# Choosing experts head by head beside the top-k, with part of the selection on GpSimd

## The chip, the cores and the metric

The kernel runs on one core of a Trainium2 chip. The metric is the device time of one execution in microseconds (us). PE is TensorE (matmuls), DVE is VectorE, ACT is ScalarE, POOL is GpSimd, and SP issues most transfers. A line number such as L541 is a line of the kernel before; where the changed kernel is quoted, the numbers are its own.

## What is computed

One decoder block on 512 tokens of width 1024, in float32: RMS norm, an input projection, a causal convolution branch and a sliding-window attention branch merged by gates, an output projection, a second RMS norm, and then a channel mixer that picks experts by product keys. The change touches that mixer only. Per token and head (8 heads) two score rows over 128 keys are formed, the best 16 of each are kept, the best 16 of the 256 sums are chosen, and the chosen experts' rows of two tables of 16,384 x 1024 are used:

```python
q = (h @ w_pq).reshape(B, S, PEER_HEADS, 2, PEER_DHALF)
sc = jnp.einsum("bshcd,hcnd->bshcn", q, sub_keys)
s_top, i_top = lax.top_k(sc, PEER_TOPK)
cand = s_top[..., 0, :, None] + s_top[..., 1, None, :]
cand_idx = i_top[..., 0, :, None] * N_KEYS + i_top[..., 1, None, :]
best, pos = lax.top_k(cand.reshape(...), PEER_TOPK)
expert_idx = jnp.take_along_axis(cand_idx.reshape(...), pos, axis=-1)
gate = jax.nn.softmax(best, axis=-1)
a = jax.nn.gelu(jnp.einsum("ced,cd->ce", u_emb[idx], hx), approximate=False)
out = jnp.einsum("ce,ced->cd", g * a, v_emb[idx])
```

## The kernel before

The 512 tokens are 4 blocks of 128 tokens, one token per partition. Block 0 gathers its experts' rows by indirect DMA from GpSimd's queue (`by_rows`, `gathered`, L600). Blocks 1 to 3 are "dense": for them all 16,384 experts are multiplied out, 128 at a time. One **up-projection** (`u_step`, L635 to L641) loads a table block of 128 experts (`wraw`), ACT rounds it to `whi` (L120), DVE forms the remainder `wlo` (L122), PE runs 24 matmuls of 384 columns (L130 to L132), and ACT takes the GELU. Of 128 up-projections 31 are due before the second table starts.

The stretch around the change has two parts.

The **top-k part** (`scores`, `head`): for each of 16 score rows (8 heads x 2) PE forms the query and the scores, and DVE finds the best 16 for the four blocks: MAX8 (L482), FIND_INDEX8 (L483), MATCH_REPLACE8 (L484), then both once more (L485, L486). After every second row `head` builds 80 candidate sums per token (`cand`, L504 to L510, two buffers) and takes their best 16: values into `bv`, positions into `bp`.

The **choosing and building part**: for each dense block `choose(b)` turns positions into experts, and `build_g(b)` writes a gate table to memory. `choose` computes from `bp`, with 11 small DVE instructions on 128 elements (8 heads x 16), which of the 16 first keys (`c_i`) and of the 16 second keys (`c_j`) each winner used. It then looks the key numbers up without a gather. It compares the position with 0 to 15 (`eq`, L539), multiplies with the key numbers (L541) and sums over 16 (`sel`, L542), on tiles of 4 heads x 16 x 16 = 1024 elements:

```python
tt(eq, src[:, hs, :, None].to_broadcast(wide), iota[...].to_broadcast(wide), op=OP.is_equal)
nc.vector.tensor_tensor(eq, eq, sif[:, hs, s, None, :].to_broadcast(wide), op=OP.mult)
nc.vector.tensor_reduce(r[:, hs], eq, axis=AX.X, op=OP.add)
```

That is 4 such triples per block, 16 in all, every one on DVE. The result gives the row index for gathers (`c_e`, `eidx`, L544 and L545) and, for dense blocks, the key numbers split into a high part, a low part and a second key, transposed into `keyT`. `build_g` then makes, per group of 16 tokens, one-hot operands on DVE (`xa`, `xb`, two `yt` at L584 and two `xt` at L587 of 1024 elements), multiplies them on PE (L592, the histogram matmuls), and ACT moves the result to `gst` (L594). A dense block has 8 groups, so there are 24. One up-projection is emitted after each group.

The order of the instructions on each engine is not the order of this text: a list scheduler with its own model of durations places every instruction when the kernel is built, keeps each engine's queue in that order, and sets the waits. So up-projections, top-k and choosing are interleaved on DVE. The pools are single or double buffered as the `bufs` say; a buffer's next writer waits for its last reader.

Of the kernel before, what the change touches and what calls it, by code (L numbers as in the profile page):

```python
# [21 lines left out]
NB = S // P  # L22
# [15 lines left out]
CAND = 80  # L38
# [13 lines left out]
LOW = 16  # L52
# [27 lines left out]
def body(ctx: ExitStack, tc: tile.TileContext, a, out):  # L80
    nc = tc.nc
# [9 lines left out]
    def psum(tag):  # L91
        return ps.tile([P, S], F32, name=tag, tag=tag, bufs=2)
# [12 lines left out]
    iota = const.tile([P, P], F32, name="iota")  # L105
# [71 lines left out]
    def chunk(b):  # L177
        return slice(b * P, (b + 1) * P)
# [223 lines left out]
    p = psum("ot")  # L402
# [4 lines left out]
    for j in range(KB):  # L407
# [4 lines left out]
        else:  # L412
            nc.scalar.activation(sq, y[:, j], AF.Square)
            nc.vector.tensor_tensor(ysum, ysum, sq, op=OP.add)
    p = psum("ot")
    nc.tensor.matmul(p, ones, ysum, start=True, stop=True)
    r = rstd_of(p, D, [fr.tile([P, S], F32, name="ln_v", tag="qs", bufs=2),
                       fr.tile([P, S], F32, name="ln_t", tag="sg"),
                       fr.tile([P, S], F32, name="ln_r", tag="qs", bufs=2)])
# [7 lines left out]
    for j in range(KB):  # L427
        p = mm_block(a["w_ao"][j], oT)
        nc.vector.tensor_tensor(sga[:, j], sga[:, j], p, op=OP.mult)
    mT = pair_y("m")  # L430
    for j in range(KB):
        p = mm_block(a["w_co"][j], yT)
# [11 lines left out]
    for b0 in range(0, NB, 2):  # L444
        acc = [psum(t) for t in (("ot", "ot", "sc", "sc") if b0 == 0 else ("sc", "sc", "mm", "mm"))]
        for k in range(KB):
            hi, lo = load_w(a["w_out"][k])
            for c in range(2):
                for n in range(2):
                    ns = slice(n * 512, (n + 1) * 512)  # L450
                    p, cs = acc[2 * c + n], chunk(b0 + c)
# [3 lines left out]
        for c in range(2):  # L455
            b = b0 + c
# [11 lines left out]
    eidx = rp.tile([P, NB, SLOTS], U32, name="eidx")  # L468
# [5 lines left out]
    rt = gctx.enter_context(tc.tile_pool(name="rt", bufs=1, reuse_waits="tile"))  # L474
    sv = rt.tile([P, NB, 16, TOPK], F32, name="sv")
    si = rt.tile([P, NB, 16, TOPK], U32, name="si")
    bv = rt.tile([P, NB, HEADS, TOPK], F32, name="bv")
    bp = rt.tile([P, NB, HEADS, TOPK], U32, name="bp")

    def top16(vals, idx, src, n):  # L480
        w = rt.tile([P, P], F32, name="topw", bufs=2)[:, :n]
        nc.vector.max(vals[:, 0:8], src)  # L482
        nc.vector.max_index(idx[:, 0:8], vals[:, 0:8], src)  # L483
        nc.vector.match_replace(w, vals[:, 0:8], src, -3.0e38)  # L484
        nc.vector.max(vals[:, 8:16], w)  # L485
        nc.vector.max_index(idx[:, 8:16], vals[:, 8:16], w)  # L486

    def scores(hc):
        if hc == 0:
            early[:] = halves([a["w_pq"][0], a["w_pq"][1]], tT)  # L490
        p = early[hc] if hc < 2 else mm_block(a["w_pq"][hc], tT)
        sk = rt.tile([P, P], F32, name="sk", bufs=2)
        nc.sync.dma_start(sk, a["subk"][hc])
        q = rt.tile([P, S], F32, name="pq", bufs=2)
        nc.scalar.activation(q, p, AF.Copy)
        p = psum("sc")
        for b in range(NB):
            nc.tensor.matmul(p[:, chunk(b)], q[:, chunk(b)], sk, start=True, stop=True)
        for b in range(NB):
            top16(sv[:, b, hc], si[:, b, hc], p[:, chunk(b)], KEYS)  # L500

    def head(h):
        s1, s2 = sv[:, :, 2 * h], sv[:, :, 2 * h + 1]
        cand = rt.tile([P, NB, CAND], F32, name="cand", bufs=2)  # L504
        nc.vector.tensor_tensor(cand[:, :, 0:16], s1[:, :, 0:1].to_broadcast([P, NB, 16]), s2, op=OP.add)
        nc.vector.tensor_tensor(cand[:, :, 16:72].rearrange("p b (i j) -> p b i j", j=8),
                                s1[:, :, 1:8, None].to_broadcast([P, NB, 7, 8]),
                                s2[:, :, None, 0:8].to_broadcast([P, NB, 7, 8]), op=OP.add)
        nc.vector.tensor_tensor(cand[:, :, 72:80], s1[:, :, 8:16], s2[:, :, 0:1].to_broadcast([P, NB, 8]),
                                op=OP.add)  # L510
        for b in range(NB):
            top16(bv[:, b, h], bp[:, b, h], cand[:, b], CAND)

    def choose(b):
        sh = [P, HEADS, TOPK]
        t = {n: rt.tile(sh, F32, name="c_" + n) for n in ("p", "q", "r", "t", "e", "i", "j")}
        u = rt.tile(sh, U32, name="c_u")
        ts, tt, stt = nc.vector.tensor_scalar, nc.vector.tensor_tensor, nc.vector.scalar_tensor_tensor
        nc.vector.tensor_copy(t["p"], bp[:, b])
        ts(u, bp[:, b], 3, None, op0=OP.logical_shift_right)  # L520
        nc.vector.tensor_copy(t["q"], u)
        ts(u, bp[:, b], 7, None, op0=OP.bitwise_and)
        nc.vector.tensor_copy(t["r"], u)
        ts(t["i"], t["q"], -1.0, 0.0, op0=OP.add, op1=OP.max)
        ts(t["t"], t["p"], -72.0, 0.0, op0=OP.add, op1=OP.max)
        tt(t["i"], t["i"], t["t"], op=OP.add)
        ts(t["t"], t["q"], 1.0, 8.0, op0=OP.is_equal, op1=OP.mult)
        stt(t["j"], t["q"], 9.0, t["r"], op0=OP.is_lt, op1=OP.mult)
        tt(t["j"], t["j"], t["t"], op=OP.add)
        sif = rt.tile([P, HEADS, 2, TOPK], F32, name="sif")  # L530
        nc.vector.tensor_copy(sif, si[:, b].rearrange("p (h c) k -> p h c k", c=2))
        wide = [P, HEADS // 2, TOPK, TOPK]
        sel = []
        for s, src in ((0, t["i"]), (1, t["j"])):
            r = rt.tile(sh, F32, name=f"sel{s}")
            for h0 in (0, HEADS // 2):
                hs = slice(h0, h0 + HEADS // 2)
                eq = rt.tile(wide, F32, name="eq")
                tt(eq, src[:, hs, :, None].to_broadcast(wide), iota[:, None, None, :TOPK].to_broadcast(wide),  # L539
                   op=OP.is_equal)  # L540
                nc.vector.tensor_tensor(eq, eq, sif[:, hs, s, None, :].to_broadcast(wide), op=OP.mult)  # L541
                nc.vector.tensor_reduce(r[:, hs], eq, axis=AX.X, op=OP.add)  # L542
            sel.append(r)
        stt(t["e"], sel[0], float(KEYS), sel[1], op0=OP.mult, op1=OP.add)  # L544
        nc.vector.tensor_copy(eidx[:, b], t["e"].rearrange("p h k -> p (h k)"))  # L545
        gt = gate[:, b].rearrange("p (h k) -> p h k", h=HEADS)
        tt(gt, bv[:, b], bv[:, b, :, 0:1].to_broadcast(sh), op=OP.subtract)
        nc.scalar.activation(gt, gt, AF.Exp)
        sm = small.tile([P, HEADS], F32, name="sm")
        nc.vector.tensor_reduce(sm, gt, axis=AX.X, op=OP.add)  # L550
        nc.vector.reciprocal(sm, sm)
        tt(gt, gt, sm[:, :, None].to_broadcast(sh), op=OP.mult)
        if b in DENSE:
            nc.vector.tensor_copy(u, sel[0])
            ts(u, u, 4, None, op0=OP.logical_shift_right)
            nc.vector.tensor_copy(t["p"], u)
            stt(t["q"], t["p"], -float(LOW), sel[0], op0=OP.mult, op1=OP.add)
            p = psum("tr")
            for s, k in enumerate((t["p"], t["q"], sel[1])):
                nc.tensor.transpose(p[:, chunk(s)], k.rearrange("p h k -> p (h k)"), ident)  # L560
            nc.scalar.activation(keyT[:, :, b], p[:, :3 * P].rearrange("p (s t) -> p s t", s=3), AF.Copy)

    def build_g(b):
        n = DENSE.index(b)
# [109 lines left out]
    for hc in range(16):  # L674
        scores(hc)
        if hc % 2:
            head(hc // 2)
    ups = iter(range(P))

    def up(n):  # L680
# [7 lines left out]
    for b in DENSE:  # L688
        choose(b)
        for _ in build_g(b):  # L690
            if left and G_U:
                up(1)
                left -= 1
    for b in ROW_CHUNKS:
        choose(b)
# [86 lines left out]
```

## Time and profile before

| what | value |
|---|---|
| time, median of 3 runs | 1880.51 us (1879.44 to 1884.98) |
| profiled execution, its own time | 1897.27 us |
| its span | 1895.5 us |
| busy over the span | PE 92%, DVE 78%, ACT 39%, POOL 18% |
| stretch from the first top-k to the first `yt` | 535.8 to 705.8 us |
| from there to the end of the last histogram matmul | 705.8 to 912.2 us |

The profile is one execution taken by the hardware profiler. "Busy" is the time in which an engine executes at least one instruction; matmuls overlap, so their unit price is read from the distance of their starts. DVE instructions overlap by some 0.08 us in the same way. The granted clock (PEclk) is given as a share of full speed. All times in a trace are counted from the start of the span.

### The profile page before, as it was taken

What the parts mean: (1) busy time and instruction counts of PE and PEld (TensorE: products, weight loads), DVE (VectorE), ACT (ScalarE), POOL (GpSimd) and SP (SyncE); (2) the same over time, 40 slices, a digit from 0 to 9 for tenths busy, and PEclk for the clock granted to TensorE, in tenths of its full rate; (3) what the DMA queues carried; (4) which work ended last, traced back from release to release, by engine and by line L of the source; (5) the groups of instructions that cost most, each with busy time, mean ns of one, the idle gap of its engine ahead of it and who ended that gap; (6) DMA issues with size and microseconds to landing.
All of it is one profiled execution on the core that took longest, in us unless ns stands there. A gap on an engine that the chain in (4) does not pass through costs nothing.

```text
span 1895.5 us, 24387 instructions
## 1 busy us (share of the span) xinstructions
PE 1749.9 (92%) x8892; PEld 1535.2 (81%) x8892; DVE 1487.4 (78%) x2765; ACT 743.8 (39%) x1083; POOL 339.3 (18%) x268
## 2 busy tenths in 40 slices
PE   6998886999999999967599999999999999999997
PEld 5876664788787899957589989898988988998776
DVE  6998799585689999998577766775767776776787
ACT  5236543643522245546333333333333333333333
POOL 0000000000000000010043332432433432433341
PEclk9999886899999999988899999999999999999999
DMA  5332110133632234544689878887878887987884
GB/s 187 118 122 67 56 46 22 52 104 124 224 109 87 93 122 170 186 157 198 210 301 325 300 264 288 292 290 271 298 252 300 317 284 250 328 295 260 294 304 158
DMA packets 148776, 385.05 MB, mean 203 GB/s; under 512 B 12208, under 2 KB 63920, under 8 KB 145584
## 3 DMA queue, kind: packets, MB, share of 16 engines
q1 hardware_dynamic: 111792, 249.26, 38.3%
q0 software_dynamic: 36864, 134.23, 19.7%
q8 instruction: 70, 1.15, 0.2%
q14 instruction: 50, 0.41, 0.1%
HBM read 350.67 MB, written 29.88 MB: 201 GB/s over the span
## 4 chain that ended last, share of the span: by engine, by line
PE 65%; DVE 15%; DMA 8%; ACT 2%; issue 1%; SPq 0%; DVEq 0%; ACTq 0%
PE mm L130 12%; PE mm L132 12%; PE mm L131 12%; DMA gl<-gd 7%; PE tr L665 2%; PE tr L666 2%; PE sc L665 2%; PE ot L665 2%; PE sc L666 2%; PE tr L664 2%; PE ot L664 2%; PE ot L666 2%; PE sc L664 2%; DVE wlo L122 2%; DVE gl L653 2%; DVE yt L584 2%
## 5 line engine op out<-in xcount | busy, mean ns | idle before, releaser
L120 ACT ACTIVATE whi<-wraw 128x1024 fp32r<-128x1024 f32 x346 | 365.0, 1056 | 620.3 <-PE mm L131 550.4
L122 DVE TENSOR_TENSOR wlo<-wraw,whi 128x1024 fp32r<-128x1024 f32 x346 | 422.1, 1220 | 135.2 <-ACT whi L120 123.6
L132 PE MATMUL mm<-tTh,wlo 128*128 128x384 f32 (+2 forms) x1168 | 402.2, 344 | 14.5 <-DVE wlo L122 14.5
L130 PE MATMUL mm<-tTh,whi 128*128 128x384 f32 (+2 forms) x1168 | 401.2, 344 | 2.5 <-DVE x L459 1.4
L131 PE MATMUL mm<-tTl,whi 128*128 128x384 f32 (+2 forms) x1168 | 400.3, 343 | 0.2 <-DVE tTl L175 0.2
L600 POOL DMA_INDIRECT row<-pu,eidx x128 | 169.3, 1323 | 948.7 <-ACT gst L594 577.6
L132 PEld LDWEIGHTS mm<-tTh,wlo 128*128 128x128 f32 x1168 | 222.6, 191 | 22.6 <-DVE wlo L122 18.1
L130 PEld LDWEIGHTS mm<-tTh,whi 128*128 128x128 f32 x1168 | 222.7, 191 | 11.8 <-ACT whi L120 3.0
L131 PEld LDWEIGHTS mm<-tTl,whi 128*128 128x128 f32 x1168 | 222.4, 190 | 8.2 <-DVE tTl L175 0.4
L600 POOL DMA_INDIRECT row<-pv,eidx x128 | 169.0, 1320 | 311.1 <-DVE acc L623 283.0
L657 ACT ACTIVATE wh<-gl 128x384 fp32r<-128x384 f32 x128 | 67.3, 526 | 337.0 <-PE ot L665 316.4
L276 DVE SCALAR_TENSOR_TENSOR yconv<-uc,pc,yconv 128x512 f32<-128x512 f32 x240 | 169.3, 743 | 0.2
L623 DVE SCALAR_TENSOR_TENSOR acc<-row,gate,acc 128x1024 f32<-128x1024 f32 x128 | 164.2, 1283 | 6.2 <-DMA acc<-x2d 4.1
L130 PE MATMUL mm<-hTh,whi 128*128 128x512 f32 (+1 forms) x352 | 143.3, 408 | 22.9 <-ACT sgc L374 15.3
L615 DVE SCALAR_TENSOR_TENSOR row<-row,hrow 128x1024 f32<-128x1024 f32 x128 | 155.4, 1220 | 9.8 <-DMA row<-pu,eidx 9.6
L653 DVE TENSOR_TENSOR gl<-gl,ga 128x384 f32<-128x384 f32 x128 | 61.7, 553 | 107.1 <-DMA gl<-gd 90.8
L131 PE MATMUL mm<-hTl,whi 128*128 128x512 f32 (+1 forms) x352 | 140.3, 399 | 0.0
L132 PE MATMUL mm<-hTh,wlo 128*128 128x512 f32 (+1 forms) x352 | 139.5, 397 | 0.0
L658 DVE TENSOR_TENSOR wl<-gl,wh 128x384 fp32r<-128x384 f32 x128 | 71.1, 556 | 71.4 <-ACT wh L657 64.6
L664 PE MATMUL tr<-whi,wh 128*128 128x512 f32 x256 | 98.1, 392 | 15.3 <-ACT wh L657 15.3
L665 PE MATMUL tr<-wlo,wh 128*128 128x512 f32 x256 | 100.8, 396 | 3.3 <-DVE wlo L122 3.3
L130 PEld LDWEIGHTS mm<-hTh,whi 128*128 128x128 f32 x352 | 70.2, 200 | 41.3 <-ACT sgc L374 17.7
(248 smaller groups left out, 2957.5 us busy)
## 6 DMA issues: line engine op xcount, KB each, us to landing
wraw<-put SPq DMA_DIRECT2D x128, 512.0 KB, 4.2
wraw<-pv SPq DMA_DIRECT2D x128, 512.0 KB, 4.9
gd<-gst SPq DMA_DIRECT2D x24, 1024.0 KB, 7.3
gl<-gd SPq DMA_DIRECT2D x16, 1536.0 KB, 11.9
wraw<-w_in SPq DMA_DIRECT2D x42, 512.0 KB, 3.6
wraw<-w_out SPq DMA_DIRECT2D x16, 512.0 KB, 3.2
wraw<-w_pq SPq DMA_DIRECT2D x16, 512.0 KB, 4.1
wraw<-w_ao SPq DMA_DIRECT2D x8, 512.0 KB, 3.2
```

Of the source, the lines that this page charges most:

```text
L120: nc.scalar.activation(hi, raw, AF.Copy)
L122: nc.vector.tensor_tensor(lo, raw, hi.bitcast(F32), op=OP.subtract)
L130: nc.tensor.matmul(p, wh[:, ks], xh[:, k], start=(k == 0), stop=False)
L131: nc.tensor.matmul(p, wh[:, ks], xl[:, k], start=False, stop=False)
L132: pace[0] = nc.tensor.matmul(p, wl[:, ks], xh[:, k], start=False, stop=(k == KB - 1))
L276: nc.vector.scalar_tensor_tensor(y[:, j], uc[:, t:t + S], w, y[:, j], op0=OP.mult, op1=OP.add)
L600: ins = nc.gpsimd.indirect_dma_start(out=r, out_offset=None, in_=table, in_offset=bass.IndirectOffsetOnAxis(ap=eidx[:, b, s:s + 1], axis=0))
L615: nc.vector.scalar_tensor_tensor(r, r, 1.0, h, op0=OP.mult, op1=OP.mult, accum_out=dots[:, s:s + 1])
L623: nc.vector.scalar_tensor_tensor(acc, r, gate[:, b, s:s + 1], acc, op0=OP.mult, op1=OP.add)
L664: nc.tensor.matmul(p, w[0][:, chunk(n)], v[0][:, ns], start=(i == 0), stop=False)
L665: nc.tensor.matmul(p, w[0][:, chunk(n)], v[1][:, ns], start=False, stop=False)
L666: pace[0] = nc.tensor.matmul(p, w[1][:, chunk(n)], v[0][:, ns], start=False, stop=(i == P - 1))
```

## The change

`choose` is split. A new function `pick(h)` is called after each `head(h)`, so 8 times, each for one head and all 4 blocks. It does the 11 small instructions on 64 elements (4 blocks x 16) and, for the two keys in turn, one comparison of 1024 elements on DVE; the multiplication and the sum are on GpSimd, and the sum is made of additions that halve the last axis (16 to 8, 4, 2, 1). The results go to a new tile `sel`. `choose(b)` keeps the softmax and the split into digits, and the row index is now formed for block 0 alone. `cand` has one buffer instead of two; `eq` has one, as before.

```diff
-        cand = rt.tile([P, NB, CAND], F32, name="cand", bufs=2)
+        cand = rt.tile([P, NB, CAND], F32, name="cand")
...
+    sel = rt.tile([P, 2, NB, HEADS, TOPK], F32, name="sel")
+    def pick(h):
+        sh = [P, NB, TOPK]
...
+        ij = [rt.tile(sh, F32, name="c_" + n, bufs=2) for n in "ij"]
...
+        wide = [P, NB, TOPK, TOPK]
+        for c in range(2):
+            eq = rt.tile(wide, F32, name="eq")
+            nc.vector.tensor_tensor(eq, ij[c][:, :, :, None].to_broadcast(wide),
+                                    iota[:, None, None, :TOPK].to_broadcast(wide), op=OP.is_equal)
+            nc.gpsimd.tensor_tensor(eq, eq, sif[:, :, c, None, :].to_broadcast(wide), op=OP.mult)
+            n = TOPK // 2
+            while n:
+                dst = sel[:, c, :, h, :, None] if n == 1 else eq[:, :, :, :n]
+                nc.gpsimd.tensor_tensor(dst, eq[:, :, :, :n], eq[:, :, :, n:2 * n], op=OP.add)
+                n //= 2
...
-        wide = [P, HEADS // 2, TOPK, TOPK]
-        sel = []
-        for s, src in ((0, t["i"]), (1, t["j"])):
-            r = rt.tile(sh, F32, name=f"sel{s}")
-            for h0 in (0, HEADS // 2):
-                hs = slice(h0, h0 + HEADS // 2)
-                eq = rt.tile(wide, F32, name="eq")
-                tt(eq, src[:, hs, :, None].to_broadcast(wide), iota[:, None, None, :TOPK].to_broadcast(wide),
-                   op=OP.is_equal)
-                nc.vector.tensor_tensor(eq, eq, sif[:, hs, s, None, :].to_broadcast(wide), op=OP.mult)
-                nc.vector.tensor_reduce(r[:, hs], eq, axis=AX.X, op=OP.add)
-            sel.append(r)
-        stt(t["e"], sel[0], float(KEYS), sel[1], op0=OP.mult, op1=OP.add)
-        nc.vector.tensor_copy(eidx[:, b], t["e"].rearrange("p h k -> p (h k)"))
...
+        else:
+            stt(t["e"], s0, float(KEYS), s1, op0=OP.mult, op1=OP.add)
+            nc.vector.tensor_copy(eidx[:, b], t["e"].rearrange("p h k -> p (h k)"))
...
             head(hc // 2)
+            pick(hc // 2)
```

The scheduler's order of the changed kernel shows three places. On POOL, the first head's two chains (the number behind a name is its buffer; L539 is the multiplication and L543 the halving additions there):

```order
L539 TENSOR_TENSOR eq_4158<-eq_4158,sif_4156 128x1024
L543 TENSOR_TENSOR eq_4158<-eq_4158 128x64x8
L543 TENSOR_TENSOR eq_4158<-eq_4158 128x64x4
L543 TENSOR_TENSOR eq_4158<-eq_4158 128x64x2
L543 TENSOR_TENSOR sel_3933<-eq_4158 128x4x16
L539 TENSOR_TENSOR eq_4165<-eq_4165,sif_4156 128x1024
```

Sixteen such chains of five stand on a queue that held nothing there before; the row gathers come behind the last of them.

On DVE in the top-k part, the changed kernel around the second comparison of the first head (`eq_4165`; MAX, MAX_INDEX and MATCH_REPLACE are the top-k instructions):

```order
L507 TENSOR_TENSOR cand_4300<-sv_3929 128x4x56
L510 TENSOR_TENSOR cand_4300<-sv_3929 128x4x8
L485 MATCH_REPLACE topw_4294<-sv_3929,sc_4271 128x128
L484 MAX_INDEX si_3930<-sv_3929,sc_4397 128x8
L487 MAX_INDEX si_3930<-sv_3929,topw_4288 128x8
L486 MAX sv_3929<-topw_4294 128x8
L537 TENSOR_TENSOR eq_4165<-c_j_4143,iota_88 128x1024
L487 MAX_INDEX si_3930<-sv_3929,topw_4294 128x8
L506 TENSOR_TENSOR cand_4300<-sv_3929 128x4x16
L122 TENSOR_TENSOR wlo_4810<-wraw_4806,whi_4808 128x1024
L533 CAST sif_4346<-si_3930 128x128
```

The comparison `eq_4165` (L537) is new here; right behind it stand one top-k instruction and then `cand`, `wlo` and a cast.

On DVE in the building part, before:

```order
L122 TENSOR_TENSOR wlo_7041<-wraw_7037,whi_7039 128x1024
L541 TENSOR_TENSOR eq_6012<-eq_6012,sif_5996 128x1024
L519 CAST c_p_6593<-bp_3932 128x128
L584 TENSOR_TENSOR yt_5633<-keyT_3919,iota_88 128x1024
L587 TENSOR_TENSOR xt_5635<-xa_5560,xb_5561 128x1024
L542 TENSOR_REDUCE sel1_6007<-eq_6012 128x64
L531 CAST sif_6612<-si_3930 128x256
L525 TENSOR_SCALAR c_t_6596<-c_p_6593 128x128
L584 TENSOR_TENSOR yt_5649<-keyT_3919,iota_88 128x1024
L587 TENSOR_TENSOR xt_5651<-xa_5560,xb_5561 128x1024
```

and in the changed kernel (L593 and L596 are `yt` and `xt` there):

```order
L122 TENSOR_TENSOR wlo_6997<-wraw_6993,whi_6995 128x1024
L593 TENSOR_TENSOR yt_5730<-keyT_3919,iota_88 128x1024
L596 TENSOR_TENSOR xt_5732<-xa_5657,xb_5658 128x1024
L593 TENSOR_TENSOR yt_5746<-keyT_3919,iota_88 128x1024
L596 TENSOR_TENSOR xt_5748<-xa_5657,xb_5658 128x1024
L122 TENSOR_TENSOR wlo_7064<-wraw_7060,whi_7062 128x1024
L585 TENSOR_TENSOR xa_5796<-keyT_3919,iota_88 128x256
```

The triples of the other blocks, which stood between `yt` and `xt`, are gone; one `wlo`, so one up-projection, stands between any two groups.

## Rows read from the trace of the kernel before

**Rows 1.** The page, busy time, share of the span and instructions of each engine.
```profile
PE 1749.9 (92%) x8892; PEld 1535.2 (81%) x8892; DVE 1487.4 (78%) x2765; ACT 743.8 (39%) x1083; POOL 339.3 (18%) x268
```

**Rows 2.** Busy time by stretch: PE, PEld, DVE, ACT, POOL, clock, DMA share, GB/s.
```profile
535.80:705.80 170.00, 163.09 (x867) 148.51 (x867) 168.09 (x885) 54.03 (x72) 0.00 (x0) 0.99 0.32 104
705.80:800.00 94.20, 94.20 (x639) 94.13 (x638) 91.43 (x110) 53.32 (x67) 0.00 (x0) 1.00 0.46 166
800.00:844.00 44.00, 27.46 (x180) 26.33 (x179) 42.81 (x54) 19.15 (x20) 0.07 (x1) 0.81 0.40 151
844.00:912.20 68.20, 49.82 (x368) 47.05 (x367) 57.12 (x59) 44.77 (x47) 6.05 (x4) 0.92 0.51 201
```

**Rows 3.** PE's longest wait, 535.8 to 912.2: us in total, times, longest.
```profile
PE sc L592 <- DVE xt L587: 32.9, 16, 7.4
```

**Rows 4.** PE in order of time: start, us, engine, line, operation, tiles, shape, count.
```profile
717.08 1.05 PE L592 MATMUL sc<-xt,yt 128*128 128x128 f32 x8
717.97 1.06 PE L592 MATMUL ot<-xt,yt 128*128 128x128 f32 x8
...
721.00 0.34 PE L131 MATMUL mm<-tTl,whi 128*128 128x384 f32 x1
...
725.16 0.33 PE L131 MATMUL mm<-tTl,whi 128*128 128x384 f32 x1
```

**Rows 5.** DVE in order of time, three stretches.
```profile
700.61 0.29 DVE L531 CAST sif<-si 128x256 f32<-128x256 uint32 x1
700.81 0.22 DVE L525 TENSOR_SCALAR c_t<-c_p 128x128 f32<-128x128 f32 x1
700.94 0.22 DVE L521 CAST c_q<-c_u 128x128 f32<-128x128 uint32 x1
...
701.82 0.29 DVE L526 TENSOR_TENSOR c_i<-c_i,c_t 128x128 f32<-128x128 f32 x1
702.02 0.29 DVE L528 SCALAR_TENSOR_TENSOR c_j<-c_q,c_r 128x128 f32<-128x128 f32 x1
...
967.78 0.56 DVE L658 TENSOR_TENSOR wl<-gl,wh 128x384 fp32r<-128x384 f32 x1 [1.17 <-ACT wh L657]
...
988.42 1.22 DVE L122 TENSOR_TENSOR wlo<-wraw,whi 128x1024 fp32r<-128x1024 f32 x1
989.56 1.22 DVE L615 SCALAR_TENSOR_TENSOR row<-row,hrow 128x1024 f32<-128x1024 f32 x1
```

**Rows 6.** Lines L541 and L542, whole span: ns min/median/max, first and last start.
```profile
L541 DVE TENSOR_TENSOR eq<-eq,sif x16: 1215/1220/1225, 680.8 to 837.7; 128x1024 f32<-128x1024 f32 x16
L542 DVE TENSOR_REDUCE sel<-eq x16: 1208/1214/1221, 682.3 to 841.1; 128x64 f32<-128x1024 f32 x16
```

**Rows 7.** DVE's groups by line, 535.8 to 705.8: busy us, mean ns.
```profile
L541 DVE TENSOR_TENSOR eq<-eq,sif 128x1024 f32<-128x1024 f32 x4 | 4.9, 1220 | 0.0
...
L542 DVE TENSOR_REDUCE sel<-eq 128x64 f32<-128x1024 f32 x4 | 4.9, 1214 | 0.0
...
L539 DVE TENSOR_TENSOR eq<-c_i,iota 128x1024 f32<-128x1024 f32 x3 | 3.7, 1219 | 0.0
...
L539 DVE TENSOR_TENSOR eq<-c_j,iota 128x1024 f32<-128x1024 f32 x2 | 2.4, 1224 | 0.0
```

**Rows 8.** Line L584 over the whole span, and its start at 844 us.
```profile
L584 DVE TENSOR_TENSOR yt<-keyT,iota x48: 1212/1220/1227, 705.8 to 907.6; 128x1024 f32<-128x1024 f32 x48
...
844.02 1.22 DVE L584 TENSOR_TENSOR yt<-keyT,iota 128x1024 f32<-128x1024 f32 x1 [1.08 <-PE ot L592]
```

**Rows 9.** POOL's memsets by line over the whole span: busy us, mean ns, idle before.
```profile
L292 POOL MEMSET uc<- 128x30 f32 x8 | 0.9, 124 | 265.3 <-DVE yconv L276 237.3 <-DVE att_es L345 27.7 <-POOLq L774 0.3
...
L774 POOL MEMSET const-float32-0.0<- 128x1 f32 x1 | 0.1, 100 | 0.2 <-issue 0.2
```

**Rows 10.** POOL in order of time, two of its indirect DMA instructions.
```profile
966.89 0.94 POOL L600 DMA_INDIRECT row<-pu,eidx  x1 [2.20 <-DVE row L615]
...
987.63 1.68 POOL L600 DMA_INDIRECT row<-pu,eidx  x1 [15.31 <-DVE row L615]
```

More of the change, by code (lines that the diff above doesn't have):

```diff
@@ L512, in head @@
             top16(bv[:, b, h], bp[:, b, h], cand[:, b], CAND)
+    def pick(h):
+        sh = [P, NB, TOPK]
+        t = {n: rt.tile(sh, F32, name="c_" + n) for n in ("p", "q", "r", "t")}
+        ij = [rt.tile(sh, F32, name="c_" + n, bufs=2) for n in "ij"]
+        u = rt.tile(sh, U32, name="c_u")
+        ts, tt, stt = nc.vector.tensor_scalar, nc.vector.tensor_tensor, nc.vector.scalar_tensor_tensor
+        nc.vector.tensor_copy(t["p"], bp[:, :, h])
+        ts(u, bp[:, :, h], 3, None, op0=OP.logical_shift_right)
+        nc.vector.tensor_copy(t["q"], u)
+        ts(u, bp[:, :, h], 7, None, op0=OP.bitwise_and)
+        nc.vector.tensor_copy(t["r"], u)
+        ts(ij[0], t["q"], -1.0, 0.0, op0=OP.add, op1=OP.max)
+        ts(t["t"], t["p"], -72.0, 0.0, op0=OP.add, op1=OP.max)
+        tt(ij[0], ij[0], t["t"], op=OP.add)
+        ts(t["t"], t["q"], 1.0, 8.0, op0=OP.is_equal, op1=OP.mult)
+        stt(ij[1], t["q"], 9.0, t["r"], op0=OP.is_lt, op1=OP.mult)
+        tt(ij[1], ij[1], t["t"], op=OP.add)
+        sif = rt.tile([P, NB, 2, TOPK], F32, name="sif", bufs=2)
+        nc.vector.tensor_copy(sif, si[:, :, 2 * h:2 * h + 2])
+        wide = [P, NB, TOPK, TOPK]
[9 more added lines that the diff above has]
+                n //= 2
@@ L514, in choose @@
     def choose(b):
         sh = [P, HEADS, TOPK]
-        t = {n: rt.tile(sh, F32, name="c_" + n) for n in ("p", "q", "r", "t", "e", "i", "j")}
-        u = rt.tile(sh, U32, name="c_u")
         ts, tt, stt = nc.vector.tensor_scalar, nc.vector.tensor_tensor, nc.vector.scalar_tensor_tensor
[L519 to L531, printed above, removed]
@@ L544, in choose @@
-        stt(t["e"], sel[0], float(KEYS), sel[1], op0=OP.mult, op1=OP.add)
-        nc.vector.tensor_copy(eidx[:, b], t["e"].rearrange("p h k -> p (h k)"))
+        t = {n: rt.tile(sh, F32, name="d_" + n) for n in ("e", "p", "q")}
+        u = rt.tile(sh, U32, name="d_u")
+        s0, s1 = sel[:, 0, b], sel[:, 1, b]
         gt = gate[:, b].rearrange("p (h k) -> p h k", h=HEADS)
@@ L553, in choose @@
         if b in DENSE:
-            nc.vector.tensor_copy(u, sel[0])
+            nc.vector.tensor_copy(u, s0)
             ts(u, u, 4, None, op0=OP.logical_shift_right)
             nc.vector.tensor_copy(t["p"], u)
-            stt(t["q"], t["p"], -float(LOW), sel[0], op0=OP.mult, op1=OP.add)
+            stt(t["q"], t["p"], -float(LOW), s0, op0=OP.mult, op1=OP.add)
             p = psum("tr")
-            for s, k in enumerate((t["p"], t["q"], sel[1])):
+            for s, k in enumerate((t["p"], t["q"], s1)):
                 nc.tensor.transpose(p[:, chunk(s)], k.rearrange("p h k -> p (h k)"), ident)
             nc.scalar.activation(keyT[:, :, b], p[:, :3 * P].rearrange("p (s t) -> p s t", s=3), AF.Copy)
+        else:
+            stt(t["e"], s0, float(KEYS), s1, op0=OP.mult, op1=OP.add)
+            nc.vector.tensor_copy(eidx[:, b], t["e"].rearrange("p h k -> p (h k)"))
     def build_g(b):
```

## The prediction

> **What bounds the kernel now.** I read the page's totals first, then busy time stretch by stretch, then the waits, then single instructions. PE is busy 92% of the span and DVE 78% [rows 1], but these shares mix stages; the change touches two. In the **top-k stage** (535.8 to 705.8 us) DVE is busy 168.1 of 170.0 us and PE 163.1; in the **building stage** PE is busy without a gap from 705.8 to 800 with DVE at 91.4 of 94.2 us; from 800 on DVE is still nearly full (42.8 of 44.0) while PE has 27.5 of 44.0; in the last stretch, to 912.2, neither is full [rows 2]. The waits say the same: in both stages together PE waited 32.9 us for DVE's `xt` [rows 3]. So DVE bounds the top-k stage, PE the first half of the building stage, DVE its end. PE's unit prices come from the spacing of its starts, since matmuls overlap: 8 histogram matmuls start 0.89 us before the next 8, and 24 up-projection matmuls lie between 721.00 and 725.16 [rows 4]. The trace records two histogram matmuls per token, so a group of 16 tokens costs PE 4 x 0.89 = 3.57 us, an up-projection 4.16 us.
>
> **The change part by part.** On DVE too I use spacing: 1.14 us for a 1024-element instruction, 0.20 us for a 128-element one with two tensors, 0.135 us for a cast or scalar instruction of 128 [rows 5].
>
> *Removed from DVE:* 16 multiplications and 16 sums of 1024 elements [rows 6], 32 x 1.14 = 36.5 us. The 16 comparisons stay, but move.
>
> *Top-k stage without any new wait.* It loses 13 wide instructions (4+4+3+2 [rows 7]), 14.8 us; two sets of small ones, 2 x (8 x 0.135 + 3 x 0.20 + 0.20) = 3.8; the index and its cast, 0.3. It gains 16 comparisons, 18.2 us; eight sets of small ones at half width (0.10 for scalar and cast, 0.14 for two-tensor instructions: estimates between half and all of what 128 elements take), 8 x (8 x 0.10 + 3 x 0.14 + 0.135) = 10.9; two more sets of high and low digits, 1.2; the index of block 0, 0.3; two `wlo` that the order puts ahead, 2.3. Together 32.9 - 18.9 = +14 us: the first `yt` at 719.8 instead of 705.8.
>
> *Building stage.* The order puts 20.6 up-projections ahead of the first histogram matmul (19.8 before), then 13.4 between the first 14 groups, and 10 groups alone. The first histogram matmul needs two `yt`, the gate product, a `wlo` and an `xt` behind the first `yt`, 5 us, and I add 2 us because the last head's GpSimd chain is no longer hidden by other top-k work: about 727, where it was 717.1 [rows 4]. Then PE bounds: 14 x 3.57 + 13.4 x 4.16 = 106 us (DVE in it: 14 x 5.3 + 13 x 1.14 = 89). Ten groups alone took from 844.0 to 909.9 before (20 `yt`, the last at 907.6 [rows 8]), 6.6 us each: 66 us. End: 727 + 106 + 66 = 899 instead of 912.2, a gain of **13 us**, not 36, because PE is full where `choose` used to fill DVE.
>
> *Added on GpSimd.* Per tile one product of 1024 elements and halving sums of 512, 256, 128 and 64: 1,984 elements, 16 tiles. The trace shows GpSimd no arithmetic. From below: a memset takes 100 ns for one element and 124 for 30 [rows 9], 0.8 ns an element for one written stream. From above: three streams (two read, one written) one after another, 2.5 ns. I take 2.0, nearer the upper end, since the nearest row reads nothing. Then the product takes 2.15 us and a chain 4.5 us, 71 us in all on an engine that is idle here [rows 2]. The Trainium skill (GPSIMD Engine Reference, "Elementwise — side-by-side cycle accounting") measures 4497 ns for such an addition of 2048 elements; by that the product is 2.25 us and the sum below 2 us worse.
>
> *New waits of DVE for the chain.* `eq` has one buffer, so each comparison waits for the chain before it. By the order 26 and 50 DVE rows lie between, 7.6 and about 15 us of work, against 4.5: nothing, but for the 2 us at the end. Behind such a wait would stand the next scores' MAX8 and `wlo`, on which PE and ACT wait.
>
> *What sharing costs.* In the rows GpSimd and DVE do not run freely side by side: an indirect DMA instruction takes 0.94 us on GpSimd while DVE is idle, 1.68 while DVE runs two-tensor instructions back to back, and those keep their 1.22 us [rows 5, 10]. So one engine waits for the other's instruction, and in those rows it is GpSimd. A DMA instruction only issues, while the new products read two tensors for their whole length; so I expect DVE to wait wherever GpSimd came first. That counts for DVE's two-tensor instructions and for casts and scalar instructions that run at twice the rate (256 elements in 0.29 us, as long as 128 with two tensors [rows 5]), not for MAX8 and its kin, which read one tensor at the plain rate. The order shows how often. Behind each comparison such an instruction follows after 0.2 to 0.6 us (`c_j`, `cand` or `wlo`) and meets the product: on average 2.15 - 0.3 = 1.85 us. The next meets the sum of 512 (1.1 us) in most tiles, 0.75 on average; a third costs some 0.35. That is 2.95 us a tile, **47 us** in 16 tiles, all in the stage that DVE bounds. With 0.8 ns it is (0.9 - 0.3) + 0.3 + 0.2 = 1.1 a tile, 18 us; with 2.5 ns 60 us; if GpSimd alone waits, nothing. The 2 us above go, since DVE comes later than the chain. PE can't give it back: its up-projections need `wlo` from the same queue. It idles more, and its clock may fall as between 800 and 844 (0.81 with PE 62% busy [rows 2]), but the 163 us of now and some 4 more, at 0.85, still fit into 231 us.
>
> The Trainium skill (SBUF — State Buffer, "Who interferes with whom") calls the shared pair an exclusive lock, taken for a whole instruction by whoever starts first, against DVE's two-SBUF-input and 2-port instructions; the sum by it is the one I make. It also infers that tensor_tensor does not hold up descriptor generation; there the trace disagrees (1.68 us against 0.94).
>
> *At nothing:* single-buffered `cand`, since its reader and writer are both on DVE; SP, which gets no new transfer, only two weight loads earlier; GpSimd's row gathers behind the chains, whose first started at 843.9 us, long after the chains end; everything behind the last histogram, which is in the same order.
>
> **Sum.** -13 - 2 saved again + 47 = +32 us. The profiled execution took 1897.3 us (span 1895.5), so it would be 1929; the median of the three runs is 16.8 us lower, and I predict for it: 1880.5 + 32 = **1912 us**. With the bounds for GpSimd the case runs from 1883 (18 - 15 = +3) to 1926 (60 - 15 = +45). What a measurement can tell from no change is about 0.3%, 5.6 us.
>
> **Rivals.**
> 1. *DVE never waits, GpSimd does* (or nobody). For it: DVE's 1.22 us stays beside the indirect DMA [rows 5, 10]. Against it: an indirect DMA instruction reads no tensor for the length of a product. It decides if DVE's instructions beside a product keep their length. Then -13: 1867. If stretched chains pass the 7.6 us gap, a few us of it go. Chance 0.20.
> 2. *GpSimd is far slower than the three streams*, 4 ns or more. The chain of 8.4 us then passes the gap of 7.6, and comparisons wait for it even if sharing cost nothing: some 22 us in 16 tiles, 1880.5 - 13 + 22 = 1890. Nothing in the rows speaks for it. Chance 0.05.
> 3. *The whole DVE saving shows*: 36.5 - 3.5 us more of small work, 1847. That needs PE to have room in the building stage; PE's 94.2 of 94.2 us speaks against it. Chance 0.05.
> 4. *The change doesn't do what it says*: the order shows all 16 chains on GpSimd beside the top-k stage, so no chance is left for it.
>
> **How the numbers follow.** My forecast has 0.70, of which 0.04 ends within 0.3% (GpSimd near its lower bound). Faster: rivals 1 and 3, less 0.01 of rival 1 that ends within 0.3%: 0.24. Slower: 0.66 + 0.05 = 0.71. Same: 0.05. The forecast's own range is 1888 to 1926. The range must reach rival 1, since 0.25 lies on that side: 1864 to 1928, which leaves out rival 3 and the ends of the others.
>
> **What would show it.** Right: `wlo`, `cand` and `c_j` in the top-k stage far longer than now (`wlo` 1.22), some by nearly a GpSimd product; MAX8 and FIND_INDEX8 unchanged; the stage longer by some 60 us; first histogram matmul near 772, last near 944; GpSimd's product near 2.2 us; then the same length to the end. Wrong: those instructions at their old length, and a first histogram matmul near 727. Comparisons that wait long for GpSimd would mean rival 2; a building stage with PE idle under DVE, rival 3.

## The result, and the profile after

The changed kernel takes **1902.15 us** (median of 4 runs, 1900.45 to 1909.18), the kernel before beside it 1879.97 (4 runs, 1875.94 to 1884.98). The ratio is 1.0124, 95% interval 1.0088 to 1.0159: slower by some 22 us.

The totals of the page hardly show it (rows 1 of before): DVE is as busy as it was, and POOL has 103 us more.

```profile
PE 1746.7 (92%) x8892; PEld 1529.6 (81%) x8892; DVE 1491.7 (79%) x2775; ACT 743.2 (39%) x1083; POOL 442.2 (23%) x348
```

The stretches do. Busy time by stretch, columns as in [rows 2]; the first one runs from the first MAX8 to the first `yt`, the others through the building stage:

```profile
531.50:759.60 228.10, 187.86 (x907) 166.88 (x906) 221.11 (x969) 57.10 (x76) 97.09 (x80) 0.90 0.25 80
759.60:850.00 90.40, 90.40 (x651) 90.33 (x649) 73.88 (x76) 59.06 (x71) 5.76 (x4) 1.00 0.58 216
850.00:880.00 30.00, 28.98 (x216) 28.81 (x216) 26.76 (x28) 20.75 (x23) 0.00 (x0) 1.00 0.57 215
880.00:932.00 52.00, 37.48 (x280) 35.25 (x278) 42.90 (x45) 34.03 (x36) 0.00 (x0) 0.93 0.43 180
```

The top-k stage takes 228.1 us where it took 170.0, and DVE is busy in 221.1 of them. Then PE has no gap until 850, and DVE has room (73.9 of 90.4 us). The histogram matmuls and the `yt` (ns min/median/max, first and last start; the last two rows are parts of the stage):

```profile
L601 PE MATMUL sc<-xt,yt x384: 271/275/421, 768.2 to 930.7; 128*128 128x128 f32 x192
L601 PE MATMUL ot<-xt,yt x384: 275/275/422, 769.1 to 931.6; 128*128 128x128 f32 x192
...
L593 DVE TENSOR_TENSOR yt<-keyT,iota x30: 1214/1222/1250, 759.6 to 871.1; 128x1024 f32<-128x1024 f32 x30
...
L593 DVE TENSOR_TENSOR yt<-keyT,iota x18: 1217/1221/1227, 876.3 to 927.3; 128x1024 f32<-128x1024 f32 x18
```

From first MAX8 to first histogram matmul, and from there to the start of the last: 181.3 + 194.7 us before, 236.7 + 163.4 after, together +24.1 us. As far as the medians tell, the change's loss lies there and nowhere else: they give +22.2. The two profiled executions differ by 3 us only because that of before was 17 us above its median: behind the start of its last histogram matmul it took 984 us, the changed kernel's 967. That stretch varies from 967 to 984 us over the profiled executions shown here, whichever kernel ran, so single executions are compared below by the two stages.

Where the 58 us of the top-k stage come from is in DVE's groups of that stage (busy us, mean ns of one, idle before):

```profile
L122 DVE TENSOR_TENSOR wlo<-wraw,whi 128x1024 fp32r<-128x1024 f32 x33 | 47.2, 1429 | 0.4 <-ACT whi L120 0.4
L483 DVE MAX8 sv<-sc 128x8 f32<-128x128 f32 x64 | 18.2, 285 | 0.0
L531 DVE TENSOR_TENSOR c_j<-c_j,c_t 128x64 f32<-128x64 f32 x8 | 14.5, 1815 | 0.0
L506 DVE TENSOR_TENSOR cand<-sv 128x64 f32<-128x64 f32 x8 | 10.8, 1347 | 0.0
...
L537 DVE TENSOR_TENSOR eq<-c_j,iota 128x1024 f32<-128x1024 f32 x8 | 9.7, 1207 | 2.8 <-POOL sel L543 2.8
...
L533 DVE CAST sif<-si 128x128 f32<-128x128 uint32 x8 | 5.2, 653 | 0.0
```

`c_j` adds 64 elements and takes 1.8 us; `cand`, of the same size, 1.35. MAX8 keeps its length. DVE in order of time at the first head's two chains shows why:

```profile
556.19 0.28 DVE L486 MAX8 sv<-topw 128x8 f32<-128x128 f32 x1
556.38 2.26 DVE L531 TENSOR_TENSOR c_j<-c_j,c_t 128x64 f32<-128x64 f32 x1
558.64 0.28 DVE L485 MATCH_REPLACE8 topw<-sv,sc 128x128 f32<-128x128 f32 x1
...
566.28 2.37 DVE L506 TENSOR_TENSOR cand<-sv 128x64 f32<-128x64 f32 x1
568.58 1.22 DVE L122 TENSOR_TENSOR wlo<-wraw,whi 128x1024 fp32r<-128x1024 f32 x1
569.72 1.29 DVE L533 CAST sif<-si 128x128 f32<-128x128 uint32 x1
```

and POOL at the same times:

```profile
556.19 2.38 POOL L539 TENSOR_TENSOR eq<-eq,sif 128x1024 f32<-128x1024 f32 x1 [293.64 <-DVE eq L537]
558.64 3.43 POOL L543 TENSOR_TENSOR eq<-eq 128x512 f32<-128x512 f32 x3
...
566.17 2.40 POOL L539 TENSOR_TENSOR eq<-eq,sif 128x1024 f32<-128x1024 f32 x1 [3.73 <-DVE eq L537]
568.65 3.56 POOL L543 TENSOR_TENSOR eq<-eq 128x512 f32<-128x512 f32 x3
```

POOL's product ends at 558.57, and DVE's `c_j`, begun 0.2 us after the product began, at 558.64. The same at 568.57 with `cand`, which ends at 568.65. Such a wait is inside the instruction's own time: the trace calls it busy. PE pays through the scores; its longest wait in the two stages (total, times, longest) is now for the score buffer `sc` that top-k still reads (24.4 us, 6.8 before), not for `xt` [rows 3]:

```profile
PE sc L499 <- DVE topw L485: 24.4, 7, 8.1
...
PE sc L601 <- DVE xt L596: 14.4, 9, 2.7
```

### The profile page after: what moved, and what is told of

Its sections match the earlier page's. It is cut to its first block, busy times and chain, and to the rows that moved or that the text cites. A ratio compares the mean times of both kernels' runs of the same rounds, so it can differ in the third digit from the quotient of the medians.

```text
span 1898.7 us, 24496 instructions
## 1 busy us (share of the span) xinstructions
PE 1746.7 (92%) x8892; PEld 1529.6 (81%) x8892; DVE 1491.7 (79%) x2775; ACT 743.2 (39%) x1083; POOL 442.2 (23%) x348
## 3 DMA queue, kind: packets, MB, share of 16 engines
q1 hardware_dynamic: 111792, 249.26, 38.5%
## 4 chain that ended last, share of the span: by engine, by line
PE 66%; DVE 17%; DMA 5%; ACT 2%; issue 1%; POOL 0%; SPq 0%; DVEq 0%; ACTq 0%
PE mm L130 12%; PE mm L132 11%; PE mm L131 11%; DMA gl<-gd 5%; PE tr L675 3%; PE tr L674 3%; PE sc L674 3%; PE sc L675 3%; PE tr L673 3%; PE ot L674 3%; PE sc L673 3%; PE ot L673 3%; PE ot L675 3%; DVE wlo L122 2%; PE sc L601 2%; PE ot L601 2%
## 5 line engine op out<-in xcount | busy, mean ns | idle before, releaser
L122 DVE TENSOR_TENSOR wlo<-wraw,whi 128x1024 fp32r<-128x1024 f32 x346 | 429.7, 1243 | 127.4 <-ACT whi L120 117.4
L609 POOL DMA_INDIRECT row<-pv,eidx x128 | 173.7, 1357 | 293.8 <-DVE acc L632 265.2
L539 POOL TENSOR_TENSOR eq<-eq,sif 128x1024 f32<-128x1024 f32 x16 | 41.6, 2601 | 387.2 <-DVE eq L537 387.2
```

The costliest lines, as they stand in the source:

```text
L122: nc.vector.tensor_tensor(lo, raw, hi.bitcast(F32), op=OP.subtract)
L609: ins = nc.gpsimd.indirect_dma_start(out=r, out_offset=None, in_=table, in_offset=bass.IndirectOffsetOnAxis(ap=eidx[:, b, s:s + 1], axis=0))
```

## The experiments

The theory: DVE's two-tensor instructions wait where a GpSimd instruction that reads SBUF tensors came first, some 38 us in the top-k stage; without that the move would gain a little. The main rival: the move itself costs the time, by its order and its many small instructions. All kernels, with the two lengths from above and the timed ratio to the kernel before:

| kernel | top-k + building, us | sum against before (376.0) | ratio, 95% interval |
|---|---|---|---|
| changed kernel | 236.7 + 163.4 | +24.1 | 1.0124 [1.0088, 1.0159] |
| e1 move only | 232.9 + 160.7 | +17.6 | 1.0081 [1.0055, 1.0107] |
| e2 GpSimd only | 192.5 + 214.7 | +31.2 | 1.0172 [1.0141, 1.0203] |
| e3 memset chains | 200.6 + 164.4 | -11.0 | 0.9957 [0.9937, 0.9978] |
| e4 chains beside | 195.9 + 193.7 | +13.6 | 1.0076 [1.0054, 1.0098] |
| e5 second product | 257.0 + 159.1 | +40.1 | 1.0213 [1.0177, 1.0249] |
| e6 one input | 221.4 + 156.7 | +2.1 | 1.0022 [0.9998, 1.0047] |
| e7 BF16 selection | 174.0 + 183.9 | -18.1 | 0.9890 [0.9863, 0.9917] |
| e9 fused selection | 171.0 + 184.4 | -20.6 | 0.9881 [0.9853, 0.9909] |
| e10 short, one input | 208.4 + 163.5 | -4.1 | 0.9999 [0.9975, 1.0024] |
| e11 short, two inputs | 214.7 + 166.8 | +5.5 | 1.0042 [1.0025, 1.0060] |

**The move alone (e1).**

```diff
-            nc.gpsimd.tensor_tensor(eq, eq, sif[:, :, c, None, :].to_broadcast(wide), op=OP.mult)
...
-                nc.gpsimd.tensor_tensor(dst, eq[:, :, :, :n], eq[:, :, :, n:2 * n], op=OP.add)
+            nc.vector.tensor_tensor(eq, eq, sif[:, :, c, None, :].to_broadcast(wide), op=OP.mult)
+            nc.vector.tensor_reduce(sel[:, c, :, h], eq, axis=AX.X, op=OP.add)
```

> The head-by-head order of the change with nothing on GpSimd: product and sum over the last axis stand on DVE again (16 products of 1.22 us and 16 reductions of 1.21 us, together 39 us more DVE work in the top-k stage than in the changed kernel). Theory (DVE waits for GpSimd's instructions on SBUF, about 38 us in the top-k stage): c_j is back at 0.22 us, cand at 0.21 us, wlo at 1.21 us; the stage is 228 - 38 + 39 = 229 us and the time 1895 to 1908 us, as with the change. Rival (the many small instructions and the order of the move itself cost the time, not GpSimd): the stage is 228 + 39 = 267 us and the time about 1940 us. Rival (DVE waits for the single eq and cand buffers): with one engine for eq that wait goes, and the small instructions keep their length in both kernels.

1899.6 us. Of DVE's groups in its top-k stage, and of its stretches:

```profile
L122 DVE TENSOR_TENSOR wlo<-wraw,whi 128x1024 fp32r<-128x1024 f32 x36 | 43.4, 1207 | 0.3 <-ACT whi L120 0.2
...
L531 DVE TENSOR_TENSOR c_j<-c_j,c_t 128x64 f32<-128x64 f32 x8 | 1.6, 197 | 0.0
```

```profile
534.90:759.00 224.10, 196.79 (x986) 176.95 (x986) 221.42 (x1002) 61.48 (x82) 0.00 (x0) 0.92 0.27 91
```

The small instructions are small again, and DVE is busy 221.4 us, as long as in the changed kernel (221.1), although it does 38.5 us of products and sums itself. What GpSimd took off, the waits put back. The comparison is not exact: the scheduler put DVE's instructions in another order here, with 36 `wlo` in the stage and not 33. Both rivals of this run fall: the stage is nowhere near 267 us, and the small instructions did not keep their length.

**The same places, without tensors read (e3).**

```diff
-            nc.gpsimd.tensor_tensor(eq, eq, sif[:, :, c, None, :].to_broadcast(wide), op=OP.mult)
...
-                nc.gpsimd.tensor_tensor(dst, eq[:, :, :, :n], eq[:, :, :, n:2 * n], op=OP.add)
+            for _ in range(5):
+                nc.gpsimd.memset(eq, 0.0)
+            nc.gpsimd.tensor_tensor(sel[:, c, :, h, :, None], eq[:, :, :, :1], eq[:, :, :, 1:2], op=OP.add)
```

> The changed kernel with GpSimd's product and first four sums replaced by five memsets of eq (which read nothing) and a last sum of 64 elements; every DVE instruction stands where it stood. It leaves the selection out: all experts of the dense blocks become those of one index, block 0 takes its row indices from the first 16 pairs. Theory (the waits are for GpSimd instructions that read SBUF): c_j and cand are back at 0.22 and 0.21 us, wlo at 1.21, at most a few us of waits of sif and other double-rate instructions stay; the top-k stage is 187 to 195 us, the time 1862 to 1872 us, faster than before. Rival (the move itself, its order and small instructions): the top-k stage stays at 220 to 228 us, the time at 1895 to 1905 us. Rival (any GpSimd instruction holds DVE up, one that only writes too): the waits shrink only as GpSimd's busy time shrinks.

1876.43 us, faster than before (1882.92 in these runs), and 26 us below the changed kernel (29 if each is measured from the kernel before that ran beside it), though GpSimd works nearly as long (83.1 against 97.1 us in the stage):

```profile
534.50:726.50 192.00, 177.13 (x908) 159.45 (x907) 185.03 (x968) 57.08 (x76) 83.13 (x96) 0.95 0.29 96
```

```profile
L122 DVE TENSOR_TENSOR wlo<-wraw,whi 128x1024 fp32r<-128x1024 f32 x33 | 40.1, 1214 | 3.0 <-ACT whi L120 3.0
...
L533 DVE CAST sif<-si 128x128 f32<-128x128 uint32 x8 | 3.6, 454 | 0.0
...
L506 DVE TENSOR_TENSOR cand<-sv 128x64 f32<-128x64 f32 x8 | 1.7, 208 | 0.0
...
L531 DVE TENSOR_TENSOR c_j<-c_j,c_t 128x64 f32<-128x64 f32 x8 | 1.7, 208 | 0.0
```

This settles it. DVE has 968 instructions in this stage and 969 in the changed kernel's, and up to the last few they stand in the same order in both traces; its busy time is 36.1 us less (221.1 - 185.0), and the stage is 36.1 us shorter (228.1 - 192.0). What still meets a memset are casts and scalar instructions, `sif` most often (0.45 us against 0.22 in e1). The time was 4 us above the range, which puts it 11 to 21 us below the kernel before; the two stages give 11.0, and the timed interval 4 to 12.

**GpSimd alone, nothing moved (e2).** Block by block as before; product and halving sums of `choose` on GpSimd.

> The other half of the change alone: experts are chosen block by block as before, with product and halving sums on GpSimd. Theory: the eq buffer is single and nothing else stands between two tiles on DVE, so each tile costs its comparison 1.2 plus the chain of about 5 us instead of 3.6 us on DVE, +2.6 us for each of 4 tiles of a block: +10 us ahead of the first yt, and up to +10 for each of the two other dense blocks where PE waits for DVE; the top-k stage up to the first choice is as before (no waits on GpSimd there), time 1888 to 1910 us. Rival (GpSimd's work costs DVE nothing and is simply taken off it, 39 us): 1850 to 1870 us.

1916.92 us: worse than the theory's range, far from the rival. The chains now stand among DVE's 1024-element instructions, and GpSimd waits in its turn; its product (ns min/median/max) and the waits in both stages:

```profile
L541 POOL TENSOR_TENSOR eq<-eq,sif x16: 2338/3280/8933, 675.6 to 847.0; 128x1024 f32<-128x1024 f32 x16
```

```profile
PE sc L596 <- DVE xt L591: 47.2, 25, 7.3
...
DVE eq L539 <- POOL sel L545: 15.1, 7, 5.3
```

The product goes up to 8.9 us, and the wait for `xt` from 32.9 [rows 3] to 47.2 us. The first histogram matmul comes 11.2 us later than before and the building stage is 20 us longer. I had priced a chain as if alone.

**Chains that nothing uses (e4).** The kernel before, plus

```diff
+    def beside(h):
+        wide = [P, NB, TOPK, TOPK]
+        for c in range(2):
+            x = rt.tile(wide, F32, name="eq")
+            nc.gpsimd.tensor_tensor(x, bv[:, :, h, :, None].to_broadcast(wide),
+                                    iota[:, None, None, :TOPK].to_broadcast(wide), op=OP.mult)
+            n = TOPK // 2
+            while n:
+                nc.gpsimd.tensor_tensor(x[:, :, :, :n], x[:, :, :, :n], x[:, :, :, n:2 * n], op=OP.add)
+                n //= 2
```

> The kernel before, with 16 GpSimd chains (a product of 1024 elements and four halving sums) that nothing uses, two after each head's top-k, into the eq slot; nothing moves on DVE. Theory: DVE's instructions wait for them as in the changed kernel, wlo and cand and whatever stands beside a chain; the top-k stage grows by 15 to 40 us (fewer two-tensor instructions stand behind each chain than in the changed kernel), the time is 1895 to 1920 us. Rival (the move itself costs the time): nothing on the path changes, 1880 us, within 0.3%.

1897.3 us, +14.4, with no instruction added on DVE. To the first `yt` the top-k stage is 14.8 us longer, just under the 15 to 40 expected; in it `wlo` and the first step of the softmax grew (1209 and 275 ns in the kernel before):

```profile
L122 DVE TENSOR_TENSOR wlo<-wraw,whi 128x1024 fp32r<-128x1024 f32 x32 | 43.4, 1357 | 1.8 <-ACT whi L120 1.8
...
L558 DVE TENSOR_TENSOR gate<-bv 128x128 f32<-128x128 f32 x4 | 3.5, 881 | 0.0
```

The presence of the chains alone makes a kernel slower.

**A second product (e5).** One line more in the changed kernel: `nc.gpsimd.tensor_tensor(eq, eq, eq, op=OP.mult)`.

> The changed kernel with one GpSimd instruction more per chain: eq times itself ahead of the real product (zeros and ones, so nothing changes in the result), another 16 instructions of about 2.4 us. Theory (DVE's instructions wait where a long GpSimd instruction on SBUF came first): more of DVE's small instructions and of wlo fall beside one, the waits (38 us in the changed kernel) grow by 8 to 25 us, and the top-k stage with them, to 236 to 253 us; the time 1910 to 1928 us. Rival (GpSimd runs beside DVE for nothing, only the last chain counts): at most 5 us more than the changed kernel, 1900 to 1907 us.

1922.44 us, the top-k stage 248.5 us to the first `yt`: within the theory's ranges. More GpSimd work costs DVE more: `wlo` is at 1.64 us on average, and instructions that were clear in the changed kernel, as the widest `cand` (0.37 us there), now wait too. The added product, `eq` times itself, took 1.89 us (median), not the 2.4 of the real one:

```profile
L122 DVE TENSOR_TENSOR wlo<-wraw,whi 128x1024 fp32r<-128x1024 f32 x35 | 57.2, 1636 | 4.6 <-ACT whi L120 4.6
...
L507 DVE TENSOR_TENSOR cand<-sv 128x224 f32<-128x224 f32 x8 | 7.5, 934 | 0.0
```

**One tensor read or two (e6, e10, e11).** e6 puts `tensor_scalar(eq[..., :n], eq[..., :n], 0.0, None, op0=OP.mult)` with n = 16, 8, 4, 2 in the place of product and sums. e10 keeps only the first of them, and e11 only the changed kernel's product; each ends with the sum of 64 elements.

> As the kernel with memsets in the place of product and sums, but with GpSimd instructions that read one tensor: eq times the number 0, of 1024, 512, 256 and 128 elements, then the sum of 64 elements. It leaves the selection out as that one does: the dense blocks' experts become those of one index, block 0 takes its rows from the first 16 pairs. Theory, first form (any GpSimd instruction that reads SBUF holds up DVE's two-tensor instructions): c_j 1 us and more, cand and wlo longer than alone, the top-k stage 210 to 228 us, the time 1888 to 1902 us. Second form (only GpSimd instructions with two tensors in SBUF do): c_j 0.21, cand 0.21, wlo 1.21 us, the top-k stage 188 to 198 us, the time 1868 to 1880 us, as with memsets.

> The chain of the one-tensor kernel cut down to one instruction of 1024 elements (eq times the number 0) and the sum of 64 elements; the selection is left out in the same way. Theory (two-tensor instructions of DVE wait for two-tensor instructions of GpSimd; what the one-tensor kernel lost against the memsets came of its long chains, nearly 7 us each): wlo 1.22 us, cand and c_j 0.21 to 0.3 us, the time 1868 to 1878 us, as with memsets. Rival (one tensor read is enough to hold DVE up, and the earlier small instructions escaped by their places): c_j or cand over 0.6 us, the time 1885 us or more.

> The same with the one instruction reading two tensors, as in the changed kernel (eq times sif, 1024 elements), then the sum of 64 elements; the selection is left out as there (four sums are missing). Theory: wlo, cand and c_j wait for the product, each for up to 2.4 us: of the 38 us of waits of the changed kernel some half, 15 to 28 us, the top-k stage 10 to 25 us longer than with one tensor, the time 1882 to 1897 us. Rival (the waits come with one tensor too): within 5 us of the kernel with one tensor.

e6 took 1885.63 us, between the two forms. Its single instructions are on average nearly as alone (`c_j` 0.30, `wlo` 1.24 us), but the test is not clean: DVE's order is another, and `c_j` came at the start of a GpSimd instruction of 1024 elements only once, where it took 0.93 us. Its chains take nearly 7 us, and DVE is idle for 17.4 us of the stage (212.4 - 195.0) against 7.0 with memsets. The trace puts 14.9 of them down to ACT's `whi`; what the chains have to do with that is not shown. e10 and e11, whose DVE orders differ in few places, are the cleaner pair: 1879.73 and 1889.75 us, 10 us apart (9.6 in the two stages). `c_j` in e10, then in e11:

```profile
L531 DVE TENSOR_TENSOR c_j<-c_j,c_t 128x64 f32<-128x64 f32 x8 | 6.0, 750 | 0.0
```

```profile
L531 DVE TENSOR_TENSOR c_j<-c_j,c_t 128x64 f32<-128x64 f32 x8 | 15.4, 1924 | 0.0
```

So a GpSimd instruction with one tensor does hold DVE up, but not for its whole length. DVE and POOL in order of time in e10:

```profile
582.00 0.82 DVE L531 TENSOR_TENSOR c_j<-c_j,c_t 128x64 f32<-128x64 f32 x1
582.75 1.21 DVE L122 TENSOR_TENSOR wlo<-wraw,whi 128x1024 fp32r<-128x1024 f32 x1
...
581.71 2.77 POOL L539 TENSOR_SCALAR eq<-eq 128x1024 f32<-128x1024 f32 x1 [11.46 <-DVE eq L537]
```

`c_j` comes through 1.1 us after POOL's start (so in all seven tiles where it stood behind one), and `wlo` runs at its full speed while POOL is still in the same instruction. With two tensors DVE waits to the end. The rival's mark for e10 (`c_j` over 0.6 us) was reached, while its time was 2 us above the theory's range and 5 below the rival's: the truth lies between. The two stages give -4.1 for e10 and -11.0 for the memsets. e11's waits, from its means against those of e3, come to 21.7 us for `c_j`, `cand` and `wlo` (29.3 in the changed kernel), inside the 15 to 28 expected; its first histogram matmul came only 6.3 us later than e10's (214.7 against 208.4), not 10 or more.

**Faster kernels (e7, e9).** If DVE's selection is to cost less, let it do less. e9, in the kernel before (in both `cand` has one buffer):

```diff
+            eq = rt.tile([P, TOPK, 2 * HEADS, TOPK], BF16, name="eq")
+            for m in range(TOPK):
+                stt(eq[:, m], ijw, float(m), sfw[:, :, m:m + 1].to_broadcast(wide), op0=OP.is_equal, op1=OP.mult)
+            for n in (8, 4, 2):
+                tt(eq[:, :n], eq[:, :n], eq[:, n:2 * n], op=OP.add)
```

> A try at a faster kernel: the kernel before (block by block, all on DVE), with the comparison, the product and the halving sums of the selection in BF16, where the numbers 0 to 127 are exact, laid out so that the innermost dimension of every operand is contiguous. Theory: if DVE takes two-tensor instructions of BF16 at twice the rate (about 0.52 ns an element), a block costs 7 to 8 us instead of 14.6; the first stands ahead of the first yt (-7 us), the two other dense ones in the stage in which PE waits for DVE (up to -7 each): 1862 to 1876 us. Rival (no double rate for these operands): the comparison and the product cost what they did, the sums a little more: 1880 to 1890 us.

> A second try: the kernel before, with comparison and product of the selection in one scalar_tensor_tensor for each of the 16 positions (256 elements, written as BF16), then halving sums in BF16 and a last one in F32. Theory: 16 x 0.35 us + 2.2 us (4 us without double rate) = 8 to 10 us a block instead of 14.6, with the gain of 5 to 7 us a block ahead of the first yt and part of that in the two other dense blocks: 1864 to 1878 us. Rival (the many small instructions cost more than their elements): 16 x 0.6 us a block, no gain, 1880 to 1888 us.

1863.56 and 1860.82 us: both faster than both kernels, e9 by 1.2% [0.9%, 1.5%] than the one before. e7 lies inside its theory's range, e9 3 us below it. A BF16 sum of 2048 elements takes as long as a float32 one of 1024; the fused instruction of 256 elements 0.42 us, not 0.35:

```profile
L539 DVE SCALAR_TENSOR_TENSOR eq<-c_ij,sif 128x256 bf16<-128x256 f32 x64 | 22.0, 420 | 0.1
L541 DVE TENSOR_TENSOR eq<-eq 128x2048 bf16<-128x2048 bf16 x4 | 4.9, 1221 | 0.0
```

## Why the prediction was right, point by point

The sign, the mechanism and the place were right; the time was 10 us too high. Some 8 of the 10 us are the building stage. That the top-k stage came out so near is partly luck: waits put too high and idle time put at nothing cancel in it.

- **Waits of DVE, 47 us.** Mis-sized: 36.1 us by e3, which keeps some waits of its own (38 if the means of the waiting instructions are summed against e1's and e3's: `c_j` 12.9, `cand` 9.1, `wlo` 7.3, `sif` 3.5, others 5.6). The step that failed is "the next meets the sum of 512, 0.75 on average": there DVE mostly came first. At 568.58 `wlo` runs in its plain 1.22 us and POOL's sums, begun 0.07 us later, take 3.56 us; the three sums of 512, 256 and 128 elements together took 2.54 to 2.59 us in four tiles and 3.40 to 3.63 in twelve. So GpSimd paid for most second meetings. A tile costs DVE 36.1 / 16 = 2.3 us, not 2.95.
- **Top-k stage without waits, +14 us.** Right as DVE's work, too low for the stage. e1 without its 36.5 us of products and sums gives 224.1 - 36.5 - 170.0 = +17.6, and three `wlo` more than the changed kernel has (3.4 us) are in that. e3 gives +22.0, with its residual waits in it. Left out was idle time: DVE idles 7.0 us of the changed kernel's stage (228.1 - 221.1) where it idled 1.9 before, and so it does with memsets. With the waits, 61 was predicted and 58.1 came, as some 14 of work, 38 of waits and 5 of idle time.
- **GpSimd's product, 2.15 us.** 2.38 us is the median, 11% longer. The chains were busy 97 us and not 71: the shortest time of each instruction already adds up to 5.0 us a chain, 80 in all, and the other 17 us are added where they meet DVE.
- **`eq` waits for the chain: nothing but the end.** Right: 2.8 us, once.
- **First histogram matmul 772, last 944.** 768.2 and 932, in an execution whose top-k stage began 4.3 us earlier than that of before (531.5 against 535.8). Counted from there the first came 236.7 us later, 236 predicted. The building stage took 164 us where 172 were predicted. Up to 876 the sum held (107.8 us against 106, with fifteen groups and not fourteen); the step "ten groups alone, 6.6 us each" was miscounted. Behind 844.0 the kernel before had 22 `yt`, so eleven groups at 6.0 us, and the changed kernel has 18 behind 876, nine groups at 6.2.
- **A gain of 13 us, not 36, if DVE did not wait.** Right in kind: PE is full from 759.6 to 850. e3, which has the move and no such waits, gains 11.0 us.
- **Behind the last histogram nothing.** Right by the medians: the two stages explain the timed difference to 2 us. The two profiled executions differ there by 17 us, in a stretch that varies as much among the other kernels.
- **Rivals.** DVE never waits (1867): excluded by `c_j` and `cand`; e3 shows what it would have given, 1876. GpSimd far slower: excluded by 2.38 us. The whole saving: excluded by PE's full stretch.

By the Trainium skill (SBUF — State Buffer, "Who interferes with whom") the port pair that DVE and GpSimd share is locked for a whole instruction; the trace agrees for two tensors on GpSimd (`c_j` ends 0.07 us behind the product), and differs for one (in e10 `c_j` comes through 1.1 us into an instruction of 2.77).

## What to carry to other kernels

Work that is moved to GpSimd beside a full DVE is not free work: count, behind each GpSimd instruction that reads two tensors, which DVE instructions with two tensors or at double rate come next, and charge them its rest. A short DVE instruction whose mean is many times its size is such a wait, though the trace calls it busy. Look first for a cheaper form on the engine that has the work: fusing comparison and product, and sums in BF16, took 1.2% where the move to GpSimd lost 1.2%.

## What the hardware showed that I had not expected

- A GpSimd `tensor_scalar` of 1024 float32 elements takes 2.77 us, longer than a product of two tensors (2.38), and yet holds DVE's two-tensor instructions up for only the first 1.1 us or so (e10). A scalar instruction on DVE that comes later in it waits for its end: in e6 `c_t`, begun 1.83 us behind the start, took 0.98 us where it takes 0.18 in e1.
- Five memsets of 1024 elements (0.95 us each) hold up no two-tensor instruction of DVE (`c_j`, `cand` 0.21 us), but the cast `sif`, which can run at double rate, takes 0.45 us instead of 0.22 (e3).
- The wait is mutual and can be long: a GpSimd product among DVE's 1024-element instructions took up to 8.93 us (e2).
